# A hybrid decoder step on one core: more ticks for side streams, query decays loaded earlier, keys projected ahead

## The chip, the cores and the metric

The kernel runs on one core of a Trainium2 chip. A core has five engines with instruction streams of their own: TensorE (PE: matmuls, their weight loads listed as PEld), VectorE (DVE), ScalarE (ACT), GpSimd (POOL) and SyncE (SP), which here issues most DMAs; ScalarE issues the weight loads. Each engine works through its own list in order and waits on semaphores for the others. The metric is device time in microseconds (us), lower is better.

## The reference

One layer of a decoder on a prompt of 1024 tokens and 8 single-token samples, D = 1024, float32:

```python
h = rmsnorm(x, norm_g)
proj = h @ w_in                  # 1024 x 7688
(aq, ak, av, abeta, aalpha, agate, bu, bv, bgate, cq, cgate, mg) = split(proj)
ya, S, buf = delta_branch(aq, ak, av, abeta, aalpha, agate, S0, ...)   # 4 heads of 128, gated delta rule
yb, vn = chunk_mlp_branch(bu, bv, bgate, ...)                           # causal 128x128 mixing
yc = memory_branch(cq, cgate, mem_k, mem_v)                             # 4 heads, 256 memory tokens
gates = sigmoid(mg.reshape(B, T, 3, D) + b_gate)
merged = gates[:, :, 0] * (ya @ w_br_a) + gates[:, :, 1] * (yb @ w_br_b) + gates[:, :, 2] * (yc @ w_br_c)
y = rmsnorm(x + merged @ w_out, final_norm_g)
```

The delta branch is a per-token recurrence S = a S + beta k (v - a S^T k)^T, evaluated in chunks (128 tokens in this kernel, 8 chunks). Each chunk needs the products k k^T and k q^T, decays exp(gc_i - gc_j), and the inverse of a unit triangular 128x128 matrix; then a chain over the chunks carries S.

## The kernel before

**Projections.** `plan_a` and `plan_c` are lists, written by hand, of projections: each takes 128 columns of w_in and produces a 128 x 1032 result, transposed (k, v, q of head i, ag = agate, bu, bv, bg = bgate, gate = one of 24 tiles of mg). A projection (`project`) has three groups of 344 tokens; a group is 24 matmuls into one of two PSUM banks `pj` (every float32 operand is split into a high and a low part, so three products over 8 tiles: `mm3`). A group's result is evacuated by ScalarE (by VectorE for bu) to SBUF; the group after the next needs that bank. The weights of the next projection are split by ScalarE (whi) and VectorE (wlo) during the current one.

**Side streams and ticks.** All else is written as Python generators, held in `Streams`. `mm3` calls `tick()` after every 6 matmuls, that is 12 times in a projection. At a tick each stream emits its instructions up to its next `yield`; `yield n` leaves out n further ticks. So the order of instructions on each engine is fixed when the program is built, and a tick is the unit in which a stream's steps are spaced: the 6 matmuls between two steps are the time that the other engines have for the earlier step. If a stream isn't far enough when the main program needs it, `run.until` ticks without matmuls.

**The streams of a head h** (`inverse_gen`, `chunks_gen`, `chain_gen`, `sample_gen`), one head after the other:
- `inverse_gen` loads E (the decay exponents, broadcast from DRAM), forms the products k k^T of the 8 chunks (L850), their decays on VectorE (L853) and ScalarE's exp of E (L857), the norms (diag, ssk), and L (L868). L's diagonal 32x32 blocks go through DRAM to a layout Lt with one block per partition (ld, Lt). It then adds `chunks_gen`, waits some ticks, and inverts the blocks on GpSimd in 31 steps (L893, L899). The result X goes back through DRAM into U (ud, L906; L910), and the rest of the inverse is built from block products on TensorE (t1 to t4, pn, p2). Then it adds the next head's `inverse_gen` and this head's `chain_gen`.
- `chunks_gen` starts once the chain of head h-1 is through ("rec"). It loads gcb (the query decays, broadcast, L961), transposes k (Kg, kd), takes exp of gcb (L974), computes nk by Newton steps, waits for q and v, copies the samples' columns (kqs, L982), forms k q^T with decays (A, L993), the queries' norms, gcb = q times decay (L1007), the queries' rsqrt, and transposes v (r).
- `chain_gen` runs over the 8 chunks: y = U^T r - ... (evacuated by VectorE, L1045), the new state S (L1048, L1051) and the output o (L1056, L1057, evacuated by ScalarE), three ticks a chunk. It sets "rec", scales o (r, L1072), transposes it and multiplies with agate ("turned").
- `sample_gen` does the 8 samples of the head (pr, ssn, kqp, and the state update with dbc). `gates_gen`, ahead of head 0, makes beta and the decays; sbb is their broadcast for the samples.
- `conv_gen` applies the causal convolution to a projected k, v or q: four steps on VectorE, then SiLU on ScalarE.

The tiles kq, vt, E, gcb, A, L have one buffer each, so the next head's data can only be written once this head's is read. The main program holds back the projections of head i+1 until head i's chunks are done:

```python
if kind in ("k", "v", "q"):
    run.until(lambda: i == 0 or ("chunks", i - 1) in done)
```

After the delta heads come the memory keys and values and the spatial branch (`plan_c`, `b_gen`), cross-attention, the three branch projections merged with the gates, and the output projection.

## Time and profile before

| what | value |
|---|---|
| runs | 1193.98 us median of 3 (1190.14 to 1197.31) |
| profiled execution | 1195.52 us, span 1193.8 us |
| instructions in the span | 19219 |
| TensorE / VectorE / ScalarE / GpSimd busy | 95% / 54% / 35% / 12% |
| mean granted TensorE clock | 0.972 |
| delta heads | about 89 to 584 us |

Read it so: TensorE is the engine that is nearly always at work; what the others do costs time only where TensorE stands still for it. The view of waits says for each engine which instruction waited and for whom; the view of stretches gives busy times and the granted clock between two points of time; the timeline gives single instructions, with the idle time ahead of each in brackets.

### The profile page before, as it was taken

The numbers are of one execution on the slowest core, as the hardware profiler recorded it, in microseconds if no ns is written. First come the engines' busy times: TensorE is split into PE (matmuls) and PEld (weight loads), VectorE is DVE, ScalarE is ACT, GpSimd is POOL, SyncE is SP. The second block draws the span as 40 slices with busy tenths as digits, with TensorE's granted clock in tenths as the row PEclk, the third lists the DMA queues.
The fourth block names the chain that finished last, engine by engine and source line by source line (L and its number), as shares of the span: only waits on it lengthen the run. The fifth ranks groups of instructions, "written<-read, shape, count | busy, mean of one in ns | idle before, by whom it ended". The sixth has DMA issues, their size and how long they took to land.

```text
span 1193.8 us, 19219 instructions
## 1 busy us (share of the span) xinstructions
PE 1129.0 (95%) x7618; PEld 1080.2 (90%) x7618; DVE 645.1 (54%) x1653; ACT 414.0 (35%) x844; POOL 145.8 (12%) x316
## 2 busy tenths in 40 slices
PE   8989798999969997999999999899999999999997
PEld 8978787999968997899999999889999999999884
DVE  5973556583735284533047632454555245786554
ACT  7344313422322232343244422454444412132332
POOL 0000420610060006200004300101011000000000
PEclk9999898999978998999999999999999999999999
DMA  9103321323122223223445453635334255663321
GB/s 367 52 36 73 128 63 56 111 80 89 25 89 89 63 77 90 62 86 114 128 164 173 139 167 134 195 106 159 108 94 130 95 190 176 205 214 105 106 90 55
DMA packets 83612, 139.87 MB, mean 117 GB/s; under 512 B 21809, under 2 KB 51729, under 8 KB 82873
## 3 DMA queue, kind: packets, MB, share of 16 engines
q1 hardware_dynamic: 70112, 98.24, 25.3%
q10 hardware_dynamic: 13408, 40.39, 11.1%
q8 instruction: 60, 0.98, 0.3%
q14 instruction: 32, 0.25, 0.1%
HBM read 107.07 MB, written 31.64 MB: 116 GB/s over the span
## 4 chain that ended last, share of the span: by engine, by line
PE 73%; DVE 11%; POOL 6%; DMA 5%; issue 2%; ACT 2%; SPq 1%; ACTq 0%; POOLq 0%; DVEq 0%
PE pj L302 41%; PE dl L302 21%; POOL X L899 3%; POOL itmp L893 3%; PE tp L225 1%; DVE xT L330 1%; DVE wlo L280 1%; DVE kq L484 1%; PE dl L1274 1%; DMA Lt<-ld 1%; PE dl L1048 1%; DVE L L868 1%; DVE vt L484 1%; PE tp L1226 1%; DMA ld<-L 1%
## 5 line engine op out<-in xcount | busy, mean ns | idle before, releaser
L302 PE MATMUL pj<-hTh,whi 128*128 128x344 f32 (+1 forms) x1384 | 273.4, 333 | 35.7 <-ACT xraw L506 19.2
L302 PE MATMUL pj<-hTh,wlo 128*128 128x344 f32 (+1 forms) x1384 | 263.1, 325 | 2.4 <-DVE wlo L280 2.4
L302 PEld LDWEIGHTS pj<-hTh,whi 128*128 128x128 f32 x1384 | 225.7, 194 | 40.9 <-ACT xraw L506 19.7
L302 PE MATMUL pj<-hTl,whi 128*128 128x344 f32 (+1 forms) x1384 | 262.6, 327 | 0.0
L302 PEld LDWEIGHTS pj<-hTl,whi 128*128 128x128 f32 x1384 | 227.4, 193 | 0.8 <-issue 0.2
L302 PEld LDWEIGHTS pj<-hTh,wlo 128*128 128x128 f32 x1384 | 224.4, 191 | 4.0 <-DVE wlo L280 2.6
L280 DVE TENSOR_TENSOR wlo<-raw,whi 128x1024 fp32r<-128x1024 f32 (+1 forms) x92 | 99.6, 1083 | 98.9 <-ACT whi L277 97.3
L277 ACT CAST whi<-raw 128x1024 fp32r<-128x1024 f32 (+1 forms) x92 | 86.1, 935 | 82.9 <-PE dl L302 67.3
L893 POOL TENSOR_TENSOR itmp<-X,Lt 128x60 f32<-128x60 f32 (+24 forms) x124 | 46.5, 375 | 287.4 <-DMA Lt<-ld 278.0
L1098 ACT COPY stg<-pj 128x344 f32<-128x344 f32 x72 | 32.2, 447 | 123.3 <-PE pj L302 123.3
L302 PE MATMUL dl<-yh,wlo 128*128 128x344 f32 x288 | 57.4, 321 | 0.0
L302 PE MATMUL dl<-yl,whi 128*128 128x344 f32 x288 | 57.0, 320 | 0.0
L302 PE MATMUL dl<-yh,whi 128*128 128x344 f32 x288 | 57.0, 320 | 0.0
L302 PEld LDWEIGHTS dl<-yh,whi 128*128 128x128 f32 x288 | 47.8, 188 | 0.0
L302 PEld LDWEIGHTS dl<-yl,whi 128*128 128x128 f32 x288 | 47.5, 188 | 0.0
L302 PEld LDWEIGHTS dl<-yh,wlo 128*128 128x128 f32 x288 | 47.5, 188 | 0.0
L1331 POOL TENSOR_TENSOR kvt<-kvt,qb 128x1024 f32<-128x1024 f32 x8 | 19.4, 2450 | 213.9 <-PE pj L302 93.3
L899 POOL TENSOR_TENSOR X<-X,itmp 128x60 f32<-128x60 f32 (+24 forms) x124 | 43.9, 354 | 9.7
L1045 DVE COPY y<-dl 128x128 f32<-128x128 f32 x32 | 9.3, 290 | 55.6 <-PE dl L1043 43.8
L1058 ACT COPY r<-dl 128x128 f32<-128x128 f32 x32 | 8.5, 266 | 79.8 <-PE dl L1057 79.8
L1514 DVE TENSOR_TENSOR stg<-dl,stg 128x344 f32<-128x344 f32 x48 | 24.7, 514 | 18.0 <-PE dl L302 18.0
L302 PE MATMUL dl<-woh,mh 128*128 128x512 f32 x128 | 31.8, 390 | 0.0
(393 smaller groups left out, 1629.3 us busy)
## 6 DMA issues: line engine op xcount, KB each, us to landing
raw<-w_tiles ACTq DMA_DIRECT2D x61, 512.0 KB, 3.7
gate<-stg SPq DMA_DIRECT2D x23, 516.0 KB, 3.2
stg<-gate SPq DMA_DIRECT2D x23, 516.0 KB, 3.8
raw<-w_br ACTq DMA_DIRECT2D x24, 256.0 KB, 3.7
x<-x_prompt SPq DMA_DIRECT2D x8, 512.0 KB
kvt<-cache_mem_k SPq DMA_DIRECT2D x16, 256.0 KB, 3.4
kvt<-cache_mem_v SPq DMA_DIRECT2D x16, 256.0 KB, 5.2
wor<-w_out SPq DMA_DIRECT2D x8, 512.0 KB
```

What stands on the lines that cost most here:

```text
L225: PE.transpose(out, in_, ident[:p, :p])
L277: S.copy(out=hi, in_=raws[i])
L280: eng.tensor_tensor(out=lo, in0=raws[i], in1=f32(hi), op=ALU.subtract)
L302: PE.matmul(out, lhsT=w, rhs=r, start=(i == 0), stop=(i == len(ops) - 1))
L330: V.scalar_tensor_tensor(out=x[:, k], in0=x[:, k], scalar=colv[:, col + k:col + k + 1], in1=r, op0=ALU.mult, op1=ALU.mult)
L484: V.scalar_tensor_tensor(out=d, in0=raw[:, j:j + T], scalar=cw[j], in1=d, op0=ALU.mult, op1=ALU.add)
L868: V.scalar_tensor_tensor(out=L[:, c], in0=L[:, c], scalar=cj[:, c:c + 1], in1=E[:, c], op0=ALU.mult, op1=ALU.mult)
L893: G.tensor_tensor(out=tm, in0=X[:, 0:m, j:j + 1].to_broadcast([P, m, n]), in1=Lt[:, j:j + 1, j + 1:32].to_broadcast([P, m, n]), op=ALU.mult,)
L899: G.tensor_tensor(out=X[:, 0:m, j + 1:32], in0=X[:, 0:m, j + 1:32], in1=tm, op=ALU.subtract)
L1098: project("gate", i, lambda n, sl, o: S.copy(out=t[:, sl], in_=o))
L1331: G.tensor_tensor(out=kts[hb], in0=kts[hb], in1=qb[:, hb * 4:hb * 4 + 4].unsqueeze(2).to_broadcast([P, 4, 2, P]), op=ALU.mult,)
L1514: V.tensor_tensor(out=sg[:, sl], in0=o, in1=sg[:, sl], op=ALU.mult)
```

## The change

- `gates_gen`: 5 instead of 3 ticks left out ahead of the cumulative sums, 12 instead of 5 ahead of the use of sbb.
- `sample_gen`: 3 instead of 1, at two places.
- `inverse_gen`: 12 instead of 8 ticks left out ahead of the inversion; its 31 steps are spread over 25 ticks instead of 15; 2 instead of 1 between the block products (four places).
- gcb: loaded by `gcb_load`: for head 0 together with E, for head h+1 right after "rec" of head h. Its exp is moved behind the queries' norms. The nk chain moves behind gcb = q times decay. Three `yield 1` of `chunks_gen` become `yield`.
- A new mark ("kq", h) is set once gcb = q times decay is emitted; the projections of k and q of the next head wait for it instead of for "chunks"; v still waits for "chunks".
- `plan_a`: bu 0 moves to head 0's list, bg 2 to head 1's, bu 3 to head 2's; one gate moves from `plan_c` into `plan_a`.

```diff
-        [... ("bv", 2), ("bv", 3), ("bg", 0)],
-        [("k", 1), ("v", 1), ("q", 1), ("bu", 0), ("ag", 1), ("bg", 1), ("bu", 1)],
-        [("k", 2), ("v", 2), ("q", 2), ("bg", 2), ("ag", 2), ("bu", 2), ("bg", 3)],
-        [("k", 3), ("bu", 3), ("v", 3), ("q", 3), ("ag", 3)] + gates(8),
+        [... ("bv", 2), ("bv", 3), ("bg", 0), ("bu", 0)],
+        [("k", 1), ("v", 1), ("q", 1), ("ag", 1), ("bg", 1), ("bu", 1), ("bg", 2)],
+        [("k", 2), ("v", 2), ("q", 2), ("ag", 2), ("bu", 2), ("bg", 3), ("bu", 3)],
+        [("k", 3), ("v", 3), ("q", 3), ("ag", 3)] + gates(9),
...
-        plan_c += gates(1) + [("kv", j)]
+        plan_c += gates(j != 4) + [("kv", j)]
... gates_gen
-        yield 3
+        yield 5
...
-        yield 5
+        yield 12
... sample_gen, twice
-        yield 1
+        yield 3
...
+    def gcb_load(h):
+        gcb = hd[h]["gcb"] = dp.tile([P, CC, P], F32, tag="gcb", name="gcb")
+        SP.dma_start(out=gcb, in_=gcd[h * CC:(h + 1) * CC]....partition_broadcast(P))
+        return gcb
... inverse_gen
         SP.dma_start(out=E, ...)
+        if not h:
+            gcb_load(h)
...
-        yield 8
+        yield 12
         for j in range(31):
...
-            if j % 2 == 1:
+            if j % 5 != 4:
                 yield
... between the block products, four times
-        yield 1
+        yield 2
... chunks_gen
-        gcb = dp.tile([P, CC, P], F32, tag="gcb", name="gcb")
-        SP.dma_start(out=gcb, ...)
+        gcb = hd[h].get("gcb") or gcb_load(h)
... k transposes
-            yield 1
-        S.activation(out=gcb, in_=gcb, func=AF.Exp)
-        nk = ...
-        yield from rsqrt_slow(nk, ssk, "nk")
-        V.tensor_tensor(out=nk, in0=nk, in1=ssk, op=ALU.mult)
+            yield
... k q products
-            yield 1
+            yield
... after the queries' norms
+        S.activation(out=gcb, in_=gcb, func=AF.Exp)
+        yield 2
         V.tensor_tensor(out=gcb, in0=qg, in1=gcb, op=ALU.mult)
+        done.add(("kq", h))
         yield
+        nk = ...
+        yield from rsqrt_slow(nk, ssk, "nk")
+        V.tensor_tensor(out=nk, in0=nk, in1=ssk, op=ALU.mult)
... chain_gen
         done.add(("rec", h))
+        if h + 1 in hd:
+            gcb_load(h + 1)
... job
-            run.until(lambda: i == 0 or ("chunks", i - 1) in done)
+            run.until(lambda: i == 0 or ("chunks" if kind == "v" else "kq", i - 1) in done)
```

## The prediction

> **What bounds the kernel now.** I read the page first, then TensorE's waits, then stretches of time with the granted clock, then the timeline round each stall.

> ```profile
> PE 1129.0 (95%) x7618; PEld 1080.2 (90%) x7618; DVE 645.1 (54%) x1653; ACT 414.0 (35%) x844; POOL 145.8 (12%) x316
> ```

> TensorE works for 95% of 1193.8 us, so only its 65 us of idling, and time at a low clock, can be won by reordering. The stretches show where both lie (width, then busy time by engine, then the granted clock):

> ```profile
> 89.00:512.00 423.00, 381.51 (x2863) 371.10 (x2862) 234.44 (x695) 133.34 (x322) 92.65 (x263) 0.94 0.27 78
> 512.00:584.00 72.00, 72.00 (x486) 71.97 (x485) 17.58 (x45) 22.36 (x52) 0.00 (x0) 1.00 0.26 94
> 139.00:145.00 6.00, 4.00 (x17) 3.94 (x18) 0.00 (x0) 2.97 (x14) 4.82 (x16) 0.58 0.51 175
> 178.00:186.00 8.00, 5.82 (x78) 5.15 (x78) 6.45 (x15) 1.27 (x4) 0.00 (x0) 0.79 0.07 18
> 204.00:210.00 6.00, 3.97 (x18) 4.00 (x19) 3.09 (x13) 2.29 (x6) 0.00 (x0) 0.72 0.14 22
> 327.00:346.00 19.00, 7.65 (x33) 7.36 (x32) 10.45 (x26) 6.43 (x7) 11.13 (x28) 0.64 0.47 143
> 360.00:372.00 12.00, 9.34 (x46) 9.08 (x44) 7.13 (x32) 5.45 (x23) 0.74 (x5) 0.72 0.34 78
> 451.00:466.00 15.00, 7.20 (x30) 6.92 (x29) 6.60 (x11) 2.82 (x6) 9.43 (x21) 0.66 0.47 141
> 486.00:494.00 8.00, 6.37 (x34) 6.12 (x34) 4.86 (x23) 2.73 (x12) 0.00 (x0) 0.79 0.40 96
> ```

> From 89 to 512 us, the four delta heads, TensorE idles 423 - 381.5 = 41.5 us; in the 72 us after, not at all. The waits of TensorE from 89 to 584 us name them, and add up to the same 41.5 (total, times, longest):

> ```profile
> PE pj L302 <- ACT xraw L506: 19.2, 2, 11.4
> PE pj L302 <- ACT stg L1120: 8.2, 2, 6.8
> PE dl L1048 <- DVE y L1045: 3.7, 2, 3.6
> PE pj L302 <- ACT agt L1116: 2.7, 1, 2.7
> PE dl L930 <- DVE pn L924: 2.2, 1, 2.2
> PE tp L742 <- DVE pr L739: 1.6, 1, 1.6
> PE tp L761 <- DVE kqp L752: 1.6, 1, 1.6
> PE tp L702 <- DVE gp L698: 1.2, 1, 1.2
> PE dl L225 <- DVE r L1072: 1.1, 2, 0.8
> ```

> **Clock.** Each larger stall is followed by slow matmuls. A granted clock of 0.72 over 6 us is 0.28 x 6 = 1.7 us of lost clock. So I get 1.7 (178), 1.7 (204), 3.4 (360) and 1.7 (486); where the idle itself was partly at the low clock I take some off: 1.5 of 2.5 (139), 2.5 of 6.8 (327), 2.5 of 5.1 (451). Together 15.0 us, an estimate. Recoverable in all: 41.5 + 15.0 = 56.5 us.

> **The ruler.** Side streams are advanced by ticks, one for every 6 matmuls:

> ```profile
> 555.17 57.22 PE pj L302 x360
> ```

> 6 x 57.22 / 360 = 0.95 us a tick, plus what the streams put on TensorE. A projection is 12 ticks, a head's seven are 84.

> **Part 1, query decays (gcb).** The largest stall, and the two transfers:

> ```profile
> 331.28 0.43 SPq L961 DMA_DIRECT2D gcb<-gcd  x1
> ...
> 338.56 1.06 ACT L974 ACTIVATE gcb<-gcb 128x1024 f32<-128x1024 f32 x1 [8.95 <-DMA gcb<-gcd]
> ...
> 340.00 2.66 PE L302 MATMUL pj<-hTh,whi 128*128 128x344 f32 x8 [11.35 <-ACT xraw L506]
> ```
> ```profile
> E<-gcd SPq DMA_DIRECT2D x4, 512.0 KB, 6.4
> ...
> gcb<-gcd SPq DMA_DIRECT2D x4, 512.0 KB, 7.3
> ```
> ```profile
> ACT gcb L974 <- DMA gcb<-gcd: 38.1, 4, 14.4
> ```

> ScalarE's exp of gcb waits for a load issued moments before, and the evacuation (xraw) that frees TensorE's bank stands behind it. That is 11.4 and 7.8 (xraw) and 6.8 (stg). After the change head 0's load goes out with E's, and the exp is 18 ticks later. For the other heads the load is issued at "rec" of the head before, on SP behind sd_prompt only, and ScalarE reaches the exp after: two key transposes (2 ticks), `yield 1` (2), two k-q products (2), two squared transposes (2 x 2) = 10 ticks, 9.5 us plus these products; the load takes 7.3. Gone: 26.0 idle and 6.5 clock = **-32.5**. The four moved nk chains are tiny VectorE operations in ticks with no conv; nothing.

> **Part 2, more ticks in the inversion.** From the Lt load to the ud store there were 9 + 15 ticks, there will be 13 + 25. The old store stood on SP waiting for GpSimd, and ScalarE's weight load and kqs went only when it had landed:

> ```profile
> 359.22 2.52 SPq L906 DMA_DIRECT2D ud<-X  x4
> ...
> 361.61 0.20 ACT L982 COPY kqs<-kq 128x16 f32<-128x16 f32 x1 [10.78 <-DMA ud<-X]
> ...
> 363.26 2.66 PE L302 MATMUL pj<-hTh,whi 128*128 128x344 f32 x8 [2.66 <-ACT agt L1116]
> ```

> Fourteen ticks are 13 us more, over the 10.8 waited: 2.7 + 3.4 clock = **-6.1**. If a store is still late, some 3 us of slack on ScalarE cover it.

> **Part 3, block products, samples, gates.** One or two more ticks cover waits of 1.2 to 2.2 us: pn 2.2 + 1.7 clock, pr and kqp 3.2 + 1.7, gp 1.2, and the 1.4 left of the stg row, which came of `as_` waiting for its broadcast (5 ticks given, now 12): **-11.4**. VectorE's E of head 0 then waits about 5 us for its load, since E's load now shares the queue with a store; bv3.1's evacuation sits behind that on ScalarE and still beats bg0.0 by about 1 us.

> **Part 4, what comes in.** Counting yields, a new head takes 75 ticks from its E load to the next (2 to the first k-k product, 5 to Lt, 13 to the inversion's first step, 25 steps, 15 to the transposes, 3+3+3+3 to the blocks, 3 to the end): loads at ticks 26, 101, 176, 251. Before it was 57, but heads 2 and 3 then waited for their keys, so k-k ran alone, after the chain of the head before. Now keys are there 9 ticks before head 2's load, and on time for head 3's. So in heads 1, 2 and 3, k-k runs between the chain's first two chunks; before only in head 1, which is the 3.6 us row:

> ```profile
> 191.08 1.37 SPq L836 DMA_DIRECT2D E<-gcd  x1
> ...
> 195.60 1.05 PE L850 MATMUL dl<-kq 128*128 128x128 f32 x8
> ...
> 197.03 1.14 DVE L853 SCALAR_TENSOR_TENSOR E<-E,gc,mask 128x128 f32<-128x128 f32 x4 [1.63 <-DMA E<-gcd]
> ...
> 199.53 1.28 DVE L484 SCALAR_TENSOR_TENSOR vt<-xraw,colv,vt 128x1024 f32<-128x1024 f32 x1
> ...
> 200.86 0.68 DVE L860 TENSOR_TENSOR diag<-L,ident 128x512 f32<-128x512 f32 x1
> ...
> 205.60 0.28 DVE L1045 COPY y<-dl 128x128 f32<-128x128 f32 x1
> ...
> 206.03 0.77 PE L1048 MATMUL dl<-y,kd 128*128 128x128 f32 x2 [3.55 <-DVE y L1045]
> ```
> ```profile
> L280 DVE TENSOR_TENSOR wlo<-raw,whi 128x1024 fp32r<-128x1024 f32 x30 | 36.7, 1223 | 49.7 <-ACT whi L277 48.1 <-DMA sd_prompt<-S 1.6
> ```

> Unhindered, TensorE reaches y's consumer 206.03 - 3.55 - 195.60 = 6.9 us after the first k-k. VectorE needs 5.0 from diag to y's end (200.86 to 205.88); before that, E, the first y and the first S end 3.6 us after k-k if E has landed. The load now has only sd_sample ahead of it on SP, three ticks earlier, so it should.
> - Head 1: no conv in these ticks (q1's ends before): 3.6 + 5.0 + 0.1 - 6.9 = 1.8; I take 1.9.
> - Head 2: the same, plus v2's SiLU ahead of the exp on ScalarE, mostly beneath diag: 2.1.
> - Head 3: two conv steps of v3 (1.3 for the second by the row; 0.9 assumed for the first, which has one operand less) and a wlo (1.2) come between, less 0.8 of idling they fill: 1.9 + 2.6 = 4.5.

> That is 8.5, plus a cold spell of 1.7 each, 13.6; minus the old passage, 3.6 + 1.7 = 5.3: **+8.3**. The lower bound is 0 (y not late), the upper 3 us more per head if E lands as late after the tick as 6.4 us allows, clock included some 12.

> **Part 5, ticks and the moved gate.** The main program waits for "kq" ahead of k. It comes 39 ticks after E's load: 140 and 215, against k2 at 144 and k3 at 228. "chunks" comes at 147 and 222, v at 156 and 240. So no `until` runs bare; the margin at k2 is four ticks. The last head ends at tick 359 of the stage's 384 (before 330 of 372). The gate adds 12 ticks here and takes 12 from the branch stage, whose spatial stream then ends 13 ticks ahead of its first use instead of 25: nothing. bu0, bg2, bu3 only change place; bu's evacuations are VectorE's and now stand ahead of the scaling of r that the chain's last transposes wait for: I take that row's 1.1 us once more, between nothing and once per head, **+1.0** rounded, and 0.4 for what I don't see.

> **Sum.** -32.5 - 6.1 - 11.4 + 8.3 + 1.4 = -40.3. The profiled execution took 1195.5, 1.5 above the median: 1195.5 - 40.3 = 1155.2. I say 1155. Less than 6 us (0.5%) either way would be no change.

> [...] Stalls of 2.2, 2.7 and 1.6 us were each followed by a low clock here (0.79, 0.72, 0.79). [...]

> **Rivals.**
> - A, forecast, 0.60: 1155 (1146 to 1163).
> - B, the chain on VectorE costs more, 0.20: E late in all three passages, convs piling up in heads 2 and 3 at further y's: +12 to +20, 1167 to 1175. For it: the 1.63 us E wait above; against: SP is free earlier.
> - C, the short stalls didn't cool the clock, 0.10: their 6.8 us stays, and heads 1 and 2 cost no clock (3.4): 1158.6.
> - D, the change doesn't do what it says, 0.05: gcb still comes late and 32.5 stays: 1188, within 0.5%. It decides if the cover of 10 ticks falls under 7.3 us or SP stands at that moment.
> - E, slower, 0.05: gcb falls behind ud's store on SP, so that the exp waits for GpSimd's inversion. The old wait for that store cost ScalarE 10.8; with gcb's 7.3 on top it is 18 us a head, three heads and their clock about 60 on top of 1155: 1215. It decides if ud (tick 146) is issued ahead of gcb (127); my count says not.

> Faster A + B + C = 0.90, same 0.05, slower 0.05. Range 1143 (no passage stalls, and 2 us of run to run) to 1175 (B's end).

> **What would show it.** TensorE idles about 11 of those 423 us instead of 41.5; the rows for xraw, stg, agt, pn, pr, kqp vanish; the row for y L1045 grows to about 8 us in three pieces, the largest in head 3; ScalarE's wait for gcb falls from 38.1 to near 0; the mean clock rises from 0.972 to about 0.985. Wrong if xraw or stg still waits over 5 us, or if VectorE's E waits for its load in heads 1 to 3.

## The result, and the profile after

The changed kernel took 1155.77 us (median of 4 runs, 1151.26 to 1157.53) against 1195.11 for the kernel before: a ratio of 0.967, with an interval of 0.963 to 0.971. Measured a second time beside other kernels it was 1151.93, again 0.967 (0.965 to 0.969). The forecast was 1155. The profiled execution took 1155.89 us, 39.6 less than that of before.

First the page's line of busy times, then two stretches of the profile of after (width, busy time by engine, granted clock). The delta heads end 40 us sooner than before, so 472 and 544 us stand where 512 and 584 stood:

```profile
PE 1120.6 (97%) x7618; PEld 1073.8 (93%) x7618; DVE 648.8 (56%) x1653; ACT 417.5 (36%) x847; POOL 138.3 (12%) x316
...
89.00:472.00 383.00, 373.85 (x2775) 366.30 (x2774) 226.17 (x657) 137.49 (x323) 85.12 (x263) 0.98 0.29 86
472.00:544.00 72.00, 71.89 (x583) 70.08 (x582) 26.68 (x83) 21.86 (x56) 0.00 (x0) 1.00 0.26 88
```

The two stretches have to be taken together, since the last head now ends later and more of its own matmuls fall into the second: with 2164 matmuls of projections (2159 before) they hold the same work as before. TensorE idles 455 - 445.74 = 9.3 us in them where it idled 41.5, and it is busy 445.7 where it was busy 453.5: 32.2 us less idling, 7.8 less time for the work, which is mostly the clock (0.94 to 0.98 in the first stretch). Together 40.0, the whole gain. The waits of TensorE from 89 to 584 us, nine rows before, are two (total, times, longest):

```profile
PE dl L1056 <- DVE y L1053: 8.5, 4, 4.2
PE dl L947 <- DVE TA L939: 0.5, 1, 0.5
```

xraw, stg, agt, pn, pr, kqp and gp are gone, and so is r. What is left is the row forecast to grow. Its pieces, from the timeline of TensorE (idle time in brackets):

```profile
215.86 0.46 PE L1056 MATMUL dl<-y,kd 128*128 128x128 f32 x2 [1.88 <-DVE y L1053]
...
313.71 0.46 PE L1056 MATMUL dl<-y,kd 128*128 128x128 f32 x2 [1.89 <-DVE y L1053]
...
318.38 0.49 PE L1056 MATMUL dl<-y,kd 128*128 128x128 f32 x2 [0.47 <-DVE y L1053]
...
413.11 0.77 PE L1056 MATMUL dl<-y,kd 128*128 128x128 f32 x2 [4.23 <-DVE y L1053]
```

1.9, 2.1 and 4.5 were worked out; 1.88, 1.89 and 4.23 came, and a fourth piece of 0.47 in head 2 that the prediction didn't have. For head 3 the timeline of VectorE shows the row of work that y (412.68) stands behind: v3's second conv step, diag, a wlo and half of L:

```profile
405.60 1.27 DVE L484 SCALAR_TENSOR_TENSOR vt<-xraw,colv,vt 128x1024 f32<-128x1024 f32 x1
...
406.93 0.69 DVE L867 TENSOR_TENSOR diag<-L,ident 128x512 f32<-128x512 f32 x1
...
409.77 1.22 DVE L280 TENSOR_TENSOR wlo<-raw,whi 128x1024 fp32r<-128x1024 f32 x1
...
411.63 1.14 DVE L875 SCALAR_TENSOR_TENSOR L<-L,cj,E 128x128 f32<-128x128 f32 x4
412.68 0.29 DVE L1053 COPY y<-dl 128x128 f32<-128x128 f32 x1
```

So the total and the largest term left were right. Whether the 40 us came from where the prediction put them, part by part, the profile of after can't say: all parts were changed at once. That is what the experiments are for.

### The profile page after: what moved, and what is told of

Its sections match the earlier page's. It is cut to its first block, busy times and chain, and to the rows that moved or that the text cites. A ratio compares the mean times of both kernels' runs of the same rounds, so it can differ in the third digit from the quotient of the medians.

```text
span 1154.1 us, 19241 instructions
## 1 busy us (share of the span) xinstructions
PE 1120.6 (97%) x7618; PEld 1073.8 (93%) x7618; DVE 648.8 (56%) x1653; ACT 417.5 (36%) x847; POOL 138.3 (12%) x316
## 3 DMA queue, kind: packets, MB, share of 16 engines
q10 hardware_dynamic: 13408, 40.39, 11.4%
## 4 chain that ended last, share of the span: by engine, by line
PE 86%; DVE 9%; ACT 3%; DMA 1%; issue 1%; SPq 0%; ACTq 0%; DVEq 0%
PE pj L302 51%; PE dl L302 22%; PE tp L225 1%; PE dl L225 1%; DVE xT L330 1%; PE dl L1284 1%; DVE vt L484 1%; DVE wlo L280 1%; PE dl L1056 1%; PE dl L992 1%; PE tp L1236 1%; PE dl L1041 1%; PE dl L1065 1%; PE dl L857 1%; PE dl L1049 1%
## 5 line engine op out<-in xcount | busy, mean ns | idle before, releaser
L302 PE MATMUL pj<-hTh,whi 128*128 128x344 f32 (+1 forms) x1384 | 269.7, 330 | 6.7 <-DVE ql L188 3.7
L302 PE MATMUL pj<-hTh,wlo 128*128 128x344 f32 (+1 forms) x1384 | 263.3, 325 | 2.4 <-DVE wlo L280 2.4
L302 PE MATMUL pj<-hTl,whi 128*128 128x344 f32 (+1 forms) x1384 | 258.6, 324 | 0.0
L302 PEld LDWEIGHTS pj<-hTh,whi 128*128 128x128 f32 x1384 | 222.8, 191 | 10.7 <-DVE ql L188 4.0
L302 PEld LDWEIGHTS pj<-hTh,wlo 128*128 128x128 f32 x1384 | 223.9, 190 | 3.8 <-DVE wlo L280 2.6
L302 PEld LDWEIGHTS pj<-hTl,whi 128*128 128x128 f32 x1384 | 225.0, 191 | 0.8 <-issue 0.2
L280 DVE TENSOR_TENSOR wlo<-raw,whi 128x1024 fp32r<-128x1024 f32 (+1 forms) x92 | 99.5, 1083 | 60.5 <-ACT whi L277 60.5
L277 ACT CAST whi<-raw 128x1024 fp32r<-128x1024 f32 (+1 forms) x92 | 86.0, 935 | 100.4 <-PE dl L302 69.2
L1108 ACT COPY stg<-pj 128x344 f32<-128x344 f32 x72 | 32.2, 447 | 114.6 <-PE pj L302 114.5
L900 POOL TENSOR_TENSOR itmp<-X,Lt 128x60 f32<-128x60 f32 (+24 forms) x124 | 40.4, 326 | 253.1 <-DMA Lt<-ld 243.7
L302 PE MATMUL dl<-yh,wlo 128*128 128x344 f32 x288 | 57.4, 321 | 0.0
L302 PE MATMUL dl<-yh,whi 128*128 128x344 f32 x288 | 57.0, 319 | 0.0
L302 PE MATMUL dl<-yl,whi 128*128 128x344 f32 x288 | 57.0, 320 | 0.0
L302 PEld LDWEIGHTS dl<-yh,whi 128*128 128x128 f32 x288 | 47.8, 188 | 0.0
L302 PEld LDWEIGHTS dl<-yl,whi 128*128 128x128 f32 x288 | 47.5, 188 | 0.0
L302 PEld LDWEIGHTS dl<-yh,wlo 128*128 128x128 f32 x288 | 47.5, 188 | 0.0
L906 POOL TENSOR_TENSOR X<-X,itmp 128x60 f32<-128x60 f32 (+24 forms) x124 | 42.3, 341 | 9.7
L1522 DVE TENSOR_TENSOR merged<-dl,stg 128x344 f32<-128x344 f32 x24 | 12.4, 516 | 34.6 <-PE dl L302 22.4
## 6 DMA issues: line engine op xcount, KB each, us to landing
raw<-w_tiles ACTq DMA_DIRECT2D x61, 512.0 KB, 3.8
x<-x_prompt SPq DMA_DIRECT2D x8, 512.0 KB, 7.2
wor<-w_out SPq DMA_DIRECT2D x8, 512.0 KB, 4.8
```

Of the source, the lines that this page charges most:

```text
L277: S.copy(out=hi, in_=raws[i])
L280: eng.tensor_tensor(out=lo, in0=raws[i], in1=f32(hi), op=ALU.subtract)
L302: PE.matmul(out, lhsT=w, rhs=r, start=(i == 0), stop=(i == len(ops) - 1))
L900: G.tensor_tensor(out=tm, in0=X[:, 0:m, j:j + 1].to_broadcast([P, m, n]), in1=Lt[:, j:j + 1, j + 1:32].to_broadcast([P, m, n]), op=ALU.mult,)
L906: G.tensor_tensor(out=X[:, 0:m, j + 1:32], in0=X[:, 0:m, j + 1:32], in1=tm, op=ALU.subtract)
L1108: project("gate", i, lambda n, sl, o: S.copy(out=t[:, sl], in_=o))
```

## The experiments

Every kernel was timed beside the kernel before. A difference to the changed kernel is the difference of the two ratios times 1193 us; the second measurement of the changed kernel has an interval of 0.002 on each side and the others 0.001 to 0.003, so 3 to 4 us are about the least that it tells. Besides the time, each verdict rests on which rows of TensorE's waits come or go.

**Part 1 alone.** The kernel before with `gcb_load` and the later exp. The nk chain moves behind gcb = q times decay with it, and a `yield 2` stands between the exp and that product; all other ticks, the plan and the mark are untouched.

```diff
+        if not h:
+            gcb_load(h)            # and after "rec" of head h: gcb_load(h + 1)
-        S.activation(out=gcb, ...)  # behind the key transposes
+        S.activation(out=gcb, ...)  # behind the queries' norms
```

> The kernel before with Part 1 alone: gcb loaded at "rec" of the head before (head 0: with E) and its exp moved behind the queries' norms; all tick counts, the plan and the mark as before. My theory (each wait has its own price): the xraw row (19.2 us) and most of the stg row (6.8 of 8.2) vanish, ScalarE's wait for gcb falls from 38.1 us to under 3, all other rows of TensorE's waits stay (agt 2.7, pn 2.2, pr 1.6, kqp 1.6, gp 1.2, y 3.7, r 1.1). Time 1195.1 - 32.5 = 1162.6, ratio 0.973. Rival 1 (the waits are linked: ScalarE's wait for gcb covered its wait for the ud store, which now stalls TensorE instead): 10 to 18 us of xraw or agt idle, 1172 to 1180. Rival 2 (Part 1 is nothing, the ticks do the work): 1190 or more.

Measured: 1165.55 us, 0.978 (0.975 to 0.981), 26.5 us faster than before. TensorE's waits from 89 to 560 us:

```profile
PE dl L928 <- DVE TA L920: 7.1, 3, 3.0
PE dl L1055 <- DVE y L1052: 3.7, 2, 3.5
PE dl L929 <- DVE T L921: 1.5, 3, 0.8
...
PE pj L302 <- ACT stg L1129: 0.6, 1, 0.6
...
PE pj L302 <- ACT xraw L506: 0.2, 1, 0.2
```

xraw (19.2) and stg (8.2) are gone, as both theories had it. Two things neither had: agt, pr, kqp, gp and r went too and pn fell to 0.3, though nothing was done for them, and a new wait came, TA, of 8.6 us with T. So 26.5 us came where 32.5 were expected. The timeline of VectorE shows what TA is, the first transpose of the block products waiting for U, which comes late because GpSimd's inversion is (its steps still run at 350.74, and the store ud goes out at 352.81):

```profile
358.57 0.43 DVE L920 STREAM_TRANSPOSE TA<-U 32x256 f32<-32x256 f32 x1 [2.67 <-DMA U<-ud]
```

**Parts 2 and 3 undone, plainly.** Two kernels: the changed one with the inversion's ticks of before (8, and `j % 2 == 1`), and the changed one with the small yields of before.

> The changed kernel with the ticks of the inversion as before (8 and 15 in place of 12 and 25). Two terms of my sum answer. Part 2: the ud store waits for GpSimd again, +2.7 us of idle and +3.4 of clock, so about +6. Part 4: counted in yields, a head takes 14 ticks less, so heads 2 and 3 (E loads at ticks 148 and 229) again wait for their keys (k-k at 170 and 254), after or at the last chunk of the chain instead of between its first two; their y waits (2.1 and 4.5) and their cold spells (1.7 each) go, -6.6 to -10. Net by my theory -4 (between -7 and +1), about 1152, with one y row piece of about 1.9 left. Rival (the passages cost what they cost wherever k-k stands, or ud's wait is larger now that ScalarE doesn't wait for gcb): +6 or more, 1162.

> The changed kernel with the yields of the gates, of the samples and between the block products as before (Part 3 undone). My theory: the rows pn (2.2), pr and kqp (1.6 each), gp (1.2) and 1.4 of stg come back with 3.4 us of clock, +11.4; but a head is 4 ticks shorter and head 0 starts 9 ticks sooner, so k-k of heads 2 and 3 (ticks 169 and 254) falls into another part of the chain: y's pieces in heads 2 and 3 change, between -8 and 0. Together +3 to +11, I say +6, 1162. Rival (short waits do not cool the clock): the rows come back without the 3.4 us, that is up to 8 us of idle at a clock of 1.00 behind them. Rival (those waits were only in the shadow of gcb's and do not come back): no row over 1 us, time at or below the changed kernel's.

Measured: 1164.42 us, 0.976 (0.974 to 0.979), some 11 us slower than the changed kernel; and 1167.76, 0.979 (0.977 to 0.982), 15 slower. Waits of TensorE, the inversion's first:

```profile
PE dl L225 <- DVE r L1082: 11.5, 2, 6.6
PE dl L1056 <- DVE y L1053: 2.4, 1, 2.4
```
```profile
PE dl L1056 <- DVE y L1053: 8.9, 3, 4.1
PE dl L225 <- DVE r L1082: 4.3, 2, 3.5
...
PE dl L937 <- DVE pn L931: 1.1, 1, 1.1
```

My sum for the first (-4) was wrong in its sign, and the second (+6) too small. y lost the pieces of heads 2 and 3, as expected, since k-k now comes at the chain's end; but there the same VectorE work stands ahead of o's scaling instead, and r costs 11.5 us. The ticks that came out moved every later step of the heads to other ticks. A kernel of this kind therefore can't be taken apart by undoing an edit alone: the shift it causes was worth more than the edit. The two isolating runs below undo the same edits and give the ticks back elsewhere.

**The exp put back, the early load kept.**

> The changed kernel with the exp of gcb put back right behind the two key transposes; the early load stays. It tells the earlier load from the later use. In heads 1 to 3 the exp is then four ticks behind its load at the latest of the two places, about 3.8 us plus the transposes, and the load takes 7.3: ScalarE waits 3 to 5 us a head (before up to 14.4) and has some 3 us of slack, so TensorE stalls 0 to 2 us in each. My theory: +3 us (0 to +8 with clock), xraw or stg rows of 1 to 5 us in all. Rival 1 (the early load alone does it, the later exp is nothing): 0. Rival 2 (only the late use does it): ScalarE's wait returns to 38 us and the 32.5 us come back, 1188.

Measured: 1151.16 us, 0.965 (0.963 to 0.968): the same as the changed kernel or a little below. In the delta stage TensorE's waits are y (8.0) and TA (0.5), nothing else. ScalarE waits 6.7 us for gcb in three heads, and TensorE nowhere waits for ScalarE:

```profile
ACT gcb L980 <- DMA gcb<-gcd: 6.7, 3, 2.8
```

The later exp, half of Part 1's edit, is not needed. (It is two ticks behind the load here, not the four of my text.)

**Part 1 left out of the whole.** gcb loaded where the chunk stream starts and its exp behind the key transposes, as before; all else changed.

> The changed kernel without Part 1: gcb is loaded where the chunk stream starts and its exp stands right behind the key transposes, as before; everything else stays changed. Where the earlier exp alone cost nothing (the run with only the exp put back), the question is whether the load's new place carries the 32.5 us. My corrected theory: in heads 1 to 3 the ticks and the mark have already moved k-k and the Lt loads ahead of "rec", so that nothing stands ahead of gcb on SP at "rec" whichever stream issues it: ScalarE's wait stays under 4 us a head; only head 0's load falls behind Lt (before 14.2 us of wait there, with 2.5 us of TensorE's idling and 1.5 of clock): +3 to +6, 1160. Rival (the parts add, as the prediction had it): ScalarE waits 38 us again and 32.5 us come back, 1188.

Measured: 1163.26 us, 0.975 (0.972 to 0.977), 9 us slower than the changed kernel; the parts do not add. Waits of TensorE and of ScalarE:

```profile
PE dl L1054 <- DVE y L1051: 8.5, 4, 4.2
PE pj L302 <- ACT stg L1126: 7.6, 1, 7.6
```
```profile
ACT gcb L978 <- DMA gcb<-gcd: 22.3, 4, 15.4
```

Of ScalarE's 22.3 us, 15.4 are head 0's, and that is the only new stall; at 7.6 us it is three times the 2.5 of my theory, whose time was 1160. The three other heads share 6.9 us, and in them gcb is no problem although it is handled as before. SP's timeline shows why, for head 2: before, and in the changed kernel.

```profile
325.29 1.82 SPq L875 DMA_DIRECT2D ld<-L  x4
328.44 1.71 SPq L881 DMA_DIRECT2D Lt<-ld  x4
...
331.28 0.43 SPq L961 DMA_DIRECT2D gcb<-gcd  x1
```
```profile
315.43 1.90 SPq L882 DMA_DIRECT2D ld<-L  x4
318.54 2.70 SPq L888 DMA_DIRECT2D Lt<-ld  x4
...
339.10 0.36 SPq L1070 DMA_DIRECT2D sd_prompt<-S  x1
339.56 0.69 SPq L834 DMA_DIRECT2D gcb<-gcd  x1
```

Before, the keys came so late that ld and Lt were issued after "rec", and gcb stood behind them on SP. With the new ticks and the earlier projection of the keys they are through some 18 us ahead of gcb. The kernel before shows the same within itself. In its head 1, ld and Lt were through at 211.8 and gcb was issued at 232.48; there the exp waited 0.5 us, where it waited 14.2, 9.0 and 14.4 in the three other heads:

```profile
236.30 1.06 ACT L974 ACTIVATE gcb<-gcb 128x1024 f32<-128x1024 f32 x1 [0.51 <-DMA gcb<-gcd]
```

**Parts 2 and 3 undone with every head kept in its place.** The inversion's 14 ticks are given back at the end of the head's stream (`yield 15`); the small yields at the end of the gates' stream (`yield 8`) and ahead of U's transposes (`yield 18` for 14). A third kernel is the changed one itself.

> The changed kernel with the inversion's ticks as before (8 and 15), but with 14 ticks added at the end of the head's stream, so that k-k and the chain of each head stand at the same ticks as in the changed kernel. It isolates GpSimd's time from the shift. Forecast of the prediction: the ud store waits on SP, ScalarE's weight load behind it, and TensorE stalls on agt: 2.7 + 3.4 of clock, +6.1. My theory now, from the run with Part 1 alone (rows TA 7.1 and T 1.5, no agt): GpSimd ends some 10 us after its last tick, U lands late, and the block products' first transposes stall TensorE 1.5 to 3 us in each of three or four heads with a cold spell each: +10 (+5 to +14), 1166, rows TA and T together 6 to 10 us, y's row as in the changed kernel.

> The changed kernel with the yields of Part 3 as before, but with the same number of ticks given back elsewhere (9 at the end of the gates' stream, 4 ahead of U's transposes), so that every head, its k-k products and its chain stand at the same ticks as in the changed kernel. It isolates Part 3's own waits from the shift that undoing it caused. Forecast of the prediction: pn 2.2, pr and kqp 1.6 each, gp 1.2 and stg 1.4 come back with 3.4 us of clock, +11.4: 1167. My theory now: in the run that undid Part 3 and let the ticks shift, only pn (1.05) and stg (0.34) of these rows came back, the rest were places where VectorE or ScalarE was late because of gcb; so +2 (+1 to +4): 1158, with pn of about 1 us and at most one more row of 1 us.

> The changed kernel itself, so that the runs beside it have their own zero: 1155.8 by the first measurement, between 1151 and 1158; y's row 8.5 us again, and the clock in the delta stage between 0.98 and 0.99. It shows how far y's pieces and the cold spells behind them repeat.

Measured: without Part 2 1157.59 us, 0.971 (0.969 to 0.972); without Part 3 1162.38, 0.974 (0.972 to 0.976); the changed kernel 1151.93, 0.967 (0.965 to 0.969). So, inside the changed kernel, Part 2 is worth some 5 us and Part 3 some 9, each give or take 3. The rows that come back, first for Part 2, then for Part 3:

```profile
PE dl L928 <- DVE TA L920: 1.8, 1, 1.8
PE dl L947 <- DVE TA L939: 1.6, 1, 1.6
```
```profile
PE pj L302 <- ACT stg L1131: 1.6, 1, 1.6
PE tp L762 <- DVE kqd L754: 1.6, 1, 1.6
...
PE dl L938 <- DVE pn L932: 0.5, 1, 0.5
PE dl L930 <- DVE T L922: 0.4, 2, 0.2
```

My second theory of Part 2 was too dear (+10): GpSimd is late in head 0 alone, where VectorE waits 5.1 us for U. My second theory of Part 3 was too cheap (+2): stg, waiting for `as_` and its broadcast, and the sample's kqd do return. Its idle time is 4.1 us. In that profile no lost clock comes on top: the granted clock is 1.00 from 112 to 120 and from 177 to 187 us, round the two stalls of 1.6 us. The rest of the 9 is not accounted for.

**Old plan, old mark.** The changed kernel with the old lists of projections; and with "chunks" as the mark for k and q.

> The changed kernel with the order of projections of before (bu 0, bg 2, bu 3 back in their old places, one gate back in the later list). By my count of ticks "kq" of head 1 is set at 140 and k 2 would start at 132: eight ticks run bare, without matmuls. My theory: one stall of TensorE ahead of k 2 of 3 to 6 us and a cold spell of 1.7 to 3.4 behind it, the rest unchanged: +5 (+3 to +9), 1161. Rival (the order of the list is neutral, since the streams' own matmuls fill the bare ticks): within 1 us of the changed kernel.

> The changed kernel with the old mark: k and q of the next head wait for "chunks" as v does. Count: "chunks" of head 1 comes at tick 147, k 2 at 144, so three bare ticks at k 2 and none elsewhere (head 2: 222 against 228). My theory: the mark is worth one stall of 0 to 2 us with its clock, +1.5; 1157. Rival (the earlier mark is what lets k-k run inside the chain and so brings y's 8.5 us): y's pieces of heads 2 and 3 shrink and the time falls by 3 or more.

Measured: 1161.67 us, 0.973 (0.970 to 0.976), 7 slower; and 1155.81, 0.968 (0.965 to 0.971), some 2 slower, which is within the spread. For the old plan the time was as expected and the reason wrong: there is no stall ahead of k 2, where by my count eight ticks run bare. VectorE is crowded elsewhere:

```profile
PE dl L1056 <- DVE y L1053: 8.5, 3, 4.8
PE dl L225 <- DVE r L1082: 3.2, 1, 3.2
```

**The passage spread out.** The one cost left, y, comes of E, diag and L standing ahead of y in two ticks. For heads 1 to 3 they are spread over seven more, placed so that a tick with a y has only short work ahead of it:

```diff
-        yield 1                      # keys are there
+        yield 2 if h else 1
... ahead of the exp of E
+        if h:
+            yield
... behind each half of diag
+            if h:
+                yield 2             # in place of one yield behind both
```

> The changed kernel with the k-k passage of heads 1 to 3 spread over seven more ticks, placed so that the ticks of the chain's y have only short VectorE work ahead of it. My theory (Part 4: VectorE's diag and E stand ahead of y in one tick): the y row (8.5 us in four pieces) goes below 1 us, the cold spells behind two of the pieces go (1.7 and 3.4), no other row takes their place; 1155.8 - 8.5 - 5.1 = 1142, I say 1143, and the last head ends some 5 ticks ahead of the stage's end. Rival (the same VectorE work only moves to another wait, as the undone inversion ticks showed for o's scaling, r: 11.5 us where y's pieces were gone): r or later y's of 5 us or more, 1152 to 1158.

Measured: 1140.56 us (median of six; one of them took 2143, for no known cause, and the other five lie between 1138.94 and 1140.87), 0.955 (0.952 to 0.958): 14 us faster than the changed kernel, and the fastest of all. Its waits of TensorE, and the stretch that holds the delta heads:

```profile
PE dl L952 <- DVE TA L944: 0.5, 1, 0.5
PE dl L225 <- DVE r L1087: 0.4, 1, 0.4
PE dl L1061 <- DVE y L1058: 0.3, 1, 0.3
```
```profile
89.00:545.00 456.00, 454.65 (x3453) 446.46 (x3452) 251.97 (x739) 167.39 (x387) 84.74 (x263) 1.00 0.29 91
```

1.35 us of idling in 456, at a clock of 1.00. Against the changed kernel's first profile 7.9 us of idling went, and with it 4.4 us of lost clock behind y's pieces. A further 1.7 us of lost clock went from 94 to 98 us (granted clock 0.57 in the changed kernel, 1.00 here), ahead of all that this edit touches. So some 12 of the 14 us are shown to be the passage's, where Part 4 had priced it at 8.5 + 5.1 = 13.6.

## Why the prediction was right, and where it was not

**The total and what it rests on.** Idling of 41.5 us and a low clock were named as all that could be won. Of the forecast's 40.3 us, 9.9 were clock (15.0 less 5.1 for the new pieces) and the rest idling, 31.8 less the 1.4 of Part 5; idling fell by 32.2 and busy time by 7.8. Most of what is short in the clock is the 1.7 us lost from 94 to 98 us, where TensorE is busy throughout and the kernel before had 1.00; no part of the sum had such a term. The sum is right because the profile of before bounded it and because Part 4's new wait was worked out.

**Part 1 (-32.5): right in kind, too large, and not its own.** Alone it was worth 26.5. The prediction let its gain stand by itself; the TA wait (8.6 us of idling) took part of it back, while agt, pr, kqp and gp went for nothing. Left out of the whole it costs 9. The difference, some 17 us, is gain that Part 1 and the other edits each bring without the other. The step that failed is the load's 7.3 us, against which the cover of 10 ticks was set (rival D too rests on it): with SP free, the exp waited 2.8 us at most (6.7 in three heads) two ticks behind its load, and in head 1 of the kernel before the exp ran 3.8 us after the load's issue. What made gcb late was ld and Lt ahead of it on SP, which the rows of SP's queue would have shown and the prediction did not quote.

**Part 2 (-6.1): size near (5, of which 3.3 are idle time in the rows), path wrong.** The forecast path was the ud store, ScalarE's weight load behind it, agt. With agt gone by Part 1 alone, what the ticks save is U's late arrival at the block products. The prediction named no such wait, although the inversion's ticks are the time in front of it.

**Part 3 (-11.4): too large; 9 in isolation,** of which the rows show 4.1: stg and one row of the samples as named, pn only 0.5, gp nothing, and none of the 3.4 us of clock. pr in the profile of before was in part a shadow of other waits: it went with Part 1 alone.

**Part 4 (+8.3 net): right, to 0.3 us in each of the three pieces.** Its clock, 5.1, came near in total only: 1.7 us behind the piece in head 1, 2.7 (0.39 x 6.89) behind the one in head 3, none in head 2. In the second profile of the same kernel it was none in head 1, 1.7 in head 2 and 1.4 in head 3. That the total fits is in part luck. The 0.9 us that head 3's sum assumed for v3's first conv step is 0.75 in the kernel before and in the changed one. The fourth piece (0.47) stands in just those three of seven profiles in which no slow clock follows head 2's stall.

```profile
212.00:222.00 10.00, 8.12 (x47) 7.86 (x46) 5.16 (x19) 5.35 (x8) 0.00 (x0) 0.83 0.28 67
310.00:316.00 6.00, 4.11 (x29) 3.86 (x28) 5.78 (x19) 3.18 (x7) 0.00 (x0) 1.00 0.30 90
...
413.11:420.00 6.89, 6.89 (x32) 6.89 (x33) 4.12 (x10) 0.54 (x3) 0.00 (x0) 0.61 0.19 40
```

The condition that I named for being wrong did occur: VectorE's E waited for its load in heads 2 and 3.

```profile
304.00 1.14 DVE L860 SCALAR_TENSOR_TENSOR E<-E,gc,mask 128x128 f32<-128x128 f32 x4 [2.30 <-DMA E<-gcd]
...
401.60 1.14 DVE L860 SCALAR_TENSOR_TENSOR E<-E,gc,mask 128x128 f32<-128x128 f32 x4 [5.31 <-DMA E<-gcd]
```

It cost nothing, since both waits ended before the first y was due: VectorE still waited 1.12 and 0.58 us for TensorE ahead of that y. Rival B, which had it cost 12 to 20, fell with that.

**Part 5 (+1.4): did not come.** The r row vanished in the changed kernel. The undone ticks (11.5) and the old plan (3.2) show that it was the right place to fear. The moved projections, which the sum put at nothing but a little r, are worth some 7 us in the changed kernel. The ledger of ticks held in its simplest test: without the earlier mark the time moves by some 2 us, within the spread. That eight bare ticks cost nothing visible was not foreseen.

**The sum by what was measured:** Part 1 alone brings 26.5, the other edits alone some 30, and both together 39, so 17 are shared. What the others bring beyond Part 1 is 13; taken out one at a time, Part 2 costs 5, Part 3 9 and the plan 7, so these overlap too. No list of single prices adds up to the gain. The forecast was right partly by luck, because errors cancelled: Parts 1 and 3 were too dear, the plan was put at nothing, r did not come, and gains were counted singly that were shared. What carried it is that all of the idling named at the start went but for y's row.

**Rivals C to E.** D and E would have shown as waits of ScalarE for gcb; there were none. C is below.

## What to carry to other kernels

When several waits are removed at once, ask of each whether it would also go with another: a stall can be the last link of one late queue, and its price, read from the profile, is then counted twice. In a kernel whose order is written in ticks, an edit's shift of all later steps can cost more than the edit (r, 11.5 us), so isolate it by giving the ticks back. And what a tick holds for the engine that evacuates matters as much as how many ticks there are: spreading some 7 us of VectorE work over seven more ticks removed 8 of the last 9 us of idling and some 4 us of lost clock behind it.

## What the hardware showed that I had not expected

A stall of 1.9 us was followed by a low clock in some executions and not in others. In the changed kernel's two profiles, the same two pieces of y (head 1, then head 2): above, 0.83 and 1.00; here, in the second profile, 1.00 and 0.83 over 10 us.

```profile
212.00:222.00 10.00, 8.12 (x57) 7.86 (x56) 5.40 (x19) 6.58 (x12) 0.00 (x0) 1.00 0.27 67
308.00:318.00 10.00, 8.11 (x47) 7.86 (x46) 9.33 (x24) 5.61 (x9) 0.00 (x0) 0.83 0.26 67
```

0.17 x 10 is 1.7 us lost. Over the seven profiles in which these two pieces stand unchanged, 8 of 14 stalls of 1.88 or 1.89 us were followed by it. The piece of 4.1 to 4.2 us in head 3 came with a spell of low clock in all seven: a granted clock of 0.66 or 0.83 over 10 us, or 0.86 over 12. That doesn't fit my 1.7 for each short stall.

```profile
213.72:217.14 3.42, 1.54 (x12) 1.31 (x11) 3.19 (x14) 2.99 (x6) 0.00 (x0) 1.00 0.00 0
217.14:220.55 3.41, 3.41 (x15) 3.41 (x14) 0.00 (x0) 0.65 (x3) 0.00 (x0) 0.50 0.56 127
309.31:312.72 3.41, 2.51 (x17) 2.22 (x16) 3.13 (x9) 2.52 (x3) 0.00 (x0) 1.00 0.49 152
312.72:316.13 3.41, 2.42 (x17) 2.46 (x18) 3.41 (x12) 1.47 (x4) 0.00 (x0) 1.00 0.03 6
```

In four more of the seven profiles (the changed kernel's second, and those without Part 1, Part 2 and Part 3) I placed the same lengths by the end of the spell at 94 us, where eight matmuls take 1.88 to 2.44 us that take 1.44 behind it. Their edges are estimates, to some 0.2 us. Of the ten stalls in these five profiles five lie whole within one length, and all five were followed by a spell; three are split, and none of them was. The other two begin at an edge, one right at it (head 1 in the second profile, at 214.0) and one 0.1 us ahead of it (head 2 without Part 2, at 315.3); neither was followed. That is what ten stalls show; what sets the clock was not shown. The edge can lie otherwise against the same stall in another execution: in head 2 it stood inside the stall in the first profile (312.72), and in the second the edges stood at 309.6 and 313.0, round a stall from 310.40 to 312.29. By the 14 stalls, one of 1.9 us costs its own length and 8/14 of 1.7, some 1.0 us, an estimate. Rival C is thus half true: in 6 of 14 cases such a stall cost no clock. Whether the spread between runs of one kernel (1151 to 1158) comes of these spells was not shown.
